# A decoder-trunk kernel: memory normalised and transposed in the input projection, attention outputs in DRAM per chunk, keys through five buffers, projection operands in a fixed order

## Chip, cores and metric

The kernel runs on one core of one Trainium2 chip. The metric is the device time of one execution in microseconds (us), lower is better.

## What is computed

One layer of a hybrid decoder over 2048 tokens of width 1024, in fp32. Cut to what matters here:

```python
mem_n = rms_norm(mem, mem_norm)                      # 256 memory tokens of width 1024
h = x + hybrid_mixer(rms_norm(x, mix_norm), ...)     # this pair of lines is stages 1, 2 and 3a
h = h + memory_cross_attention(rms_norm(h, cross_norm), mem_n, ...)   # stage 3
h = h + hierarchical_moe(rms_norm(h, moe_norm), ...)                  # stage 4
out = rms_norm(h, final_norm)

def hybrid_mixer(h, ...):
    fq, fk, fv, ff, gq, gk, gv, gg, ga = split(h @ w_in)
    fox = rms_norm(forgetting_attention(fq, fk, fv, ff + b_forget), fox_out_gain)   # 8 heads x 64, causal softmax
    gla = rms_norm(gla_chunked(gq, gk, gv, log_a), gla_out_gain) * silu(gg)         # 4 heads
    return concat(fox, gla) @ w_out

def memory_cross_attention(h, mem_n, ...):
    q, k, v = h @ w_xq, mem_n @ w_xk, mem_n @ w_xv
    return softmax(q k / sqrt(128)) v @ w_xo
```

## The kernel before

Fp32 products are made of fp32r halves: `split` (L58 to L72) writes a rounded part hi on ScalarE (ACT: L68, or L71 with a scale) and the rest lo on VectorE (DVE: L69, or L72), and `mm3` (L88 to L92) makes hi by hi, lo by hi and hi by lo on TensorE (PE: L90, L91, L92). A Tile scheduler sets the order of each engine's instructions; `issue_after` and `keep_in_program_order` bind it in places.

**Stage 1** (`stage1`, L129) normalises and transposes x in four chunks of 512 tokens (`prenorm`, and `turn` with its PE transposes L214), and multiplies by column groups of `w_in`: GQ and GK first, chunk by chunk with the next chunk's `turn` between the products, then GG, GV, FV, FQ and FK. From FV on the gated linear attention runs between them. FQ and FK end in `ttype` (L158): a PSUM tile `ps_mm` is split into two SBUF tiles from one ring of three (`tag="o1"`, L166), and four stores on SyncE's DMA queue (SP, L170) write the hi and lo of two heads to the DRAM tiles `qh_d`, `ql_d`, `kh_d`, `kl_d` of the chunk. The last group is FK, the keys.

**Stage 2** (`stage2`, L473) is the attention, in 16 units: p is a pair of heads, c a chunk of 512 queries. `load` (L492) fetches a unit's q and k halves (six DMAs of 256 to 272 KB) and, where p is 0, 256 KB of v; for p = 0 and c < 3 they are issued on GpSimd's queue (POOL), else on SP. `v1`, the 1 MB of v for the second pair, is always POOL's (L511). `maxima` (L513) finds each query's largest score: PE products `ps_a` (L525 and L526), DVE reductions (L528, and L530 for the diagonal block), a transpose `pmt` (L536), and a split of the negated maxima into `mh` and `ml`, which two POOL DMAs (L540) put into two rows of `q2`, in SBUF. `probs` then forms scores minus maxima (`ps_b`, L569 and L570, the second needs the rows just written), exponentials on ACT (L572) and the products with v. A unit's normalised output goes to the DRAM tensor `yT_d` (L620). In the last four units the generator `memory_in` (L771) runs beside them: it loads the gain broadcast over 128 partitions (L776) and two halves of the memory (L779), forms the sum of squares on ACT (L783), scales on DVE (L785), transposes on PE (L792) and copies to `mT` on DVE (L793).

**Stage 3a** (L685, `mixed` L701) is the output projection. Eight row blocks of `w_out` are loaded on SP (`wst`, L692) and split into `woh` (ACT) and `wol` (DVE). `enter(i)` loads 128 tokens of attention output `yT` (L719) and of gated linear attention output `y` (L720) and splits them into `yh` and `yl`; tile 0's loads are POOL's. `memory_out` (L803) forms the memory's keys (`ps_m`, L813) in between.

## Time and profile before

| | |
|---|---|
| runs | 2441.82, 2445.04, 2445.13 us, median 2445.04 |
| profiled execution | 2442.03 us, of which the span is 2440.3 us |
| PE busy | 2321.5 us, 95% of the span |
| DVE, ACT, POOL busy | 1433.6, 953.7, 678.7 us |
| granted clock of PE, mean over the span | 0.977 |
| DMA moved | 337.81 MB |

The span is what the profiler sees from the first to the last instruction; the profiled execution is 1.7 us longer. PE is busy nearly everywhere, so the table by itself tells little: what matters is where PE stands idle, what ended the idle time, and at what granted clock it went on (1.00 is 2.4 GHz, 0.50 is 1.2 GHz).

### The profile page before, as it was taken

To read this page: it belongs to the slowest core of one execution; us is meant where nothing else is said; L and a number is where in the kernel's file an instruction comes from. 1 tells how busy PE (TensorE), PEld (TensorE's weight loads), DVE (VectorE), ACT (ScalarE), POOL (GpSimd) and SP (SyncE) were. 2 spreads that over 40 slices of the span, in tenths; PEclk is the share of its full clock that TensorE was granted. 3 is DMA by queue.
4 is the path that set the end of the run, shared out by engine and by line. 5 is a ranking of instruction groups with operands and counts; after the bars stand their busy time and mean duration, and the time that the engine had idled before them with its cause. 6 is when DMAs were issued, how large, how long until landed. Compare 5 with 4: busy or idle time off the path is not lost. (4 is left out here: it accounts for less than half of the span.)

```text
span 2440.3 us, 39272 instructions
## 1 busy us (share of the span) xinstructions
PE 2321.5 (95%) x14569; PEld 1873.1 (77%) x14569; DVE 1433.6 (59%) x3561; ACT 953.7 (39%) x2058; POOL 678.7 (28%) x776
## 2 busy tenths in 40 slices
PE   7999999999979999999899999999599999999996
PEld 5778887777756656565488888887499989889985
DVE  5430035656527867877642255666568868778775
ACT  5321023434312434444431154554345545454542
POOL 2000002222134666665600001111332334223132
PEclk9999999999988999999999999999799999999998
DMA  5221222444484132312273422111678788779883
GB/s 181 72 90 66 77 83 83 127 111 133 109 204 98 49 92 63 83 42 77 70 245 115 143 82 70 49 40 56 184 242 265 229 286 248 260 215 274 262 246 116
DMA packets 281972, 337.81 MB, mean 138 GB/s; under 512 B 33766, under 2 KB 203296, under 8 KB 281775
## 3 DMA queue, kind: packets, MB, share of 16 engines
q1 hardware_dynamic: 248223, 246.73, 33.6%
q0 software_dynamic: 31248, 84.32, 11.8%
q10 hardware_dynamic: 2304, 4.20, 0.5%
q8 instruction: 116, 1.90, 0.3%
q14 instruction: 81, 0.66, 0.1%
HBM read 252.27 MB, written 93.02 MB: 141 GB/s over the span
## 5 line engine op out<-in xcount | busy, mean ns | idle before, releaser
L90 PE MATMUL gu<-xTh,wer 128*128 128x288 f32 x1024 | 304.7, 302 | 0.5 <-issue 0.5
L91 PE MATMUL gu<-xTl,wer 128*128 128x288 f32 x1024 | 304.1, 298 | 0.3 <-DVE xTl L69 0.3
L92 PE MATMUL gu<-xTh,wer 128*128 128x288 f32 x1024 | 303.1, 297 | 0.0
L69 DVE TENSOR_TENSOR wer<-wes,wer 128x1024 fp32r<-128x1024 f32 x192 | 232.5, 1222 | 37.1 <-ACT wer L68 36.9
L68 ACT ACTIVATE wer<-wes 128x1024 fp32r<-128x1024 f32 x192 | 197.9, 1052 | 118.5 <-PE yd L92 43.9
L572 ACT ACTIVATE pT<-ps_b 128x512 f32<-128x512 f32 (+3 forms) x320 | 158.8, 532 | 181.7 <-PE ps_b L570 161.8
L90 PEld LDWEIGHTS gu<-xTh,wer 128*128 128x128 f32 x1024 | 193.2, 190 | 3.7 <-ACT xTh L68 0.9
L91 PEld LDWEIGHTS gu<-xTl,wer 128*128 128x128 f32 x1024 | 194.2, 190 | 2.3 <-DVE xTl L69 0.9
L92 PEld LDWEIGHTS gu<-xTh,wer 128*128 128x128 f32 x1024 | 194.1, 190 | 1.8
L591 POOL TENSOR_TENSOR l<-l,pT 128x512 f32<-128x512 f32 (+3 forms) x128 | 153.6, 1200 | 53.9 <-ACT pT L572 47.5
L90 PE MATMUL ps_mm<-xh,w1r 128*128 128x512 f32 x384 | 153.4, 402 | 0.8 <-ACT w1r L71 0.5
L91 PE MATMUL ps_mm<-xl,w1r 128*128 128x512 f32 x384 | 153.4, 400 | 0.0
L92 PE MATMUL ps_mm<-xh,w1r 128*128 128x512 f32 x384 | 152.5, 399 | 0.1
L528 DVE TENSOR_REDUCE mm<-ps_a 128x1 f32<-128x512 f32 x192 | 128.2, 683 | 38.2 <-PE ps_a L526 37.6
L91 PE MATMUL ps_mm<-w1r,xh 128*128 128x512 f32 x384 | 150.1, 393 | 0.0
L92 PE MATMUL ps_mm<-w1r,xl 128*128 128x512 f32 x384 | 149.8, 392 | 0.0
L90 PE MATMUL ps_mm<-w1r,xh 128*128 128x512 f32 x384 | 148.3, 392 | 0.3 <-ACT o L186 0.3
L525 PE MATMUL ps_a<-k,q 128*128 128x512 f32 (+2 forms) x320 | 128.7, 404 | 18.9 <-DVE o L72 9.5
L556 PE MATMUL po<-pT,v 128*64 128x512 f32 (+3 forms) x640 | 131.7, 555 | 3.0 <-POOL pT L575 2.9
L569 PE MATMUL ps_b<-q,k 128*128 128x512 f32 (+3 forms) x320 | 125.2, 398 | 2.4 <-ACT pT L572 2.4
L591 DVE TENSOR_TENSOR l<-l,pT 128x512 f32<-128x512 f32 (+3 forms) x128 | 111.7, 873 | 23.3 <-ACT pT L572 11.6
L570 PE MATMUL ps_b<-q,k 68*128 68x512 f32 (+3 forms) x320 | 116.8, 376 | 4.1 <-DMA q<-ml 4.1
(431 smaller groups left out, 5622.0 us busy)
## 6 DMA issues: line engine op xcount, KB each, us to landing
wes<-in_w_expert_down_dram SPq DMA_DIRECT2D x64, 512.0 KB
wes<-in_w_expert_gate_dram SPq DMA_DIRECT2D x62, 512.0 KB
wes<-in_w_expert_up_dram SPq DMA_DIRECT2D x62, 512.0 KB
yr_d<-ye SPq DMA_DIRECT2D x32, 512.0 KB
w1s<-in_w_in_dram SPq DMA_DIRECT2D x48, 256.0 KB
xt<-in_x_dram SPq DMA_DIRECT2D x16, 512.0 KB
h_d<-x POOLq DMA_DIRECT2D x16, 512.0 KB
h<-h_d SPq DMA_DIRECT2D x16, 512.0 KB
```

Source lines behind the costliest of these rows:

```text
L68: nc.scalar.activation(hi, src, AF.Copy)
L69: nc.vector.tensor_tensor(lo, src, f32(hi), OP.subtract)
L90: mm(ps, ah, bh, start=start, stop=False)
L91: mm(ps, ah, bl, start=False, stop=False)
L92: mm(ps, al, bh, start=False, stop=stop)
L525: nc.tensor.matmul(ps[:, :w], q1[:, i, qs], k1[:, i, :w], start=True, stop=False)
L528: nc.vector.tensor_reduce(mm[:, i, b, j:j + 1], ps[:, :w], AX.X, OP.max)
L556: ins = nc.tensor.matmul(po[i * 64:i * 64 + 64, off:], V[p][:, kb, i * 64:i * 64 + 64], pts[i][:, off:], start=new and o == 0, stop=len(to ...
L569: nc.tensor.matmul(ps[:, off:], k1[:, i, ks], q1[:, i, off:], start=True, stop=False)
L570: nc.tensor.matmul(ps[:, off:], k2[0:68, i, ks], q2[0:68, i, off:], start=False, stop=True)
L572: nc.scalar.activation(pt[:, off:], ps[:, off:], AF.Exp)
L591: add(sums[i][:, off:], sums[i][:, off:], pt[:, off:], OP.add)
```

## The change

1. The memory is normalised in stage 1, beside the products of GQ and GK for the last chunk (`memory_norm`): the same sums of squares, a scaling without the gain, the same 16 transposes into the PSUM ring of `turn`, and 16 ACT copies of 128x128 that multiply by the gain as a column; four stores write `mT_d` in DRAM. In stage 2 `memory_in` is one load of `mT`.
2. `yT_d` is four DRAM tiles, one for each chunk of queries. The last unit writes its own from POOL. Tile 0's loads of stage 3a go to SP.
3. For the keys alone, lo takes a tile of the ring `w1s` (two), and hi keeps the ring `o1` (three).
4. The loads of the unit p = 0, c = 2 move from POOL to SP, and with them the 256 KB pieces of v for c = 2 and 3.
5. In stage 3a the weights 0 to 3 are split first, then the attention half of tile 0; the keys of the memory, the weights 4 to 7 and the other half of tile 0 are ordered behind it on ACT and DVE.

```diff
@@ stage1, ttype
-                    hi, lo = (op[0].tile([128, 512], F32R, tag="o1", name="o1", bufs=3) for _ in range(2))
+                    hi = op[0].tile([128, 512], F32R, tag="o1", name="o1", bufs=3)
+                    lo = wp.tile([128, 512], F32R, tag="w1s", name="o1", bufs=2) if parts[0] is self.kh_d else \
+                        op[0].tile([128, 512], F32R, tag="o1", name="o1", bufs=3)
@@ stage1, GQ and GK
-                    tn = turn(c + 1) if c < 3 else iter(())
+                    tn = turn(c + 1) if c < 3 else self.memory_norm(ip, px, lambda: op[0].tile([128, 512], F32, tag="o1", name="o1", bufs=n_o[0]))
@@ stage2, load
-                issue = nc.sync.dma_start if p or c == 3 else nc.gpsimd.dma_start
+                issue = nc.sync.dma_start if p or c > 1 else nc.gpsimd.dma_start
...
-                    nc.gpsimd.dma_start(V[p][:, b], self.fv_d[...])
+                    (issue if p == 0 else nc.gpsimd.dma_start)(V[p][:, b], self.fv_d[...])
@@ stage2, probs
-                nc.scalar.dma_start(self.yT_d[p * 128:p * 128 + 128, c * 512:(c + 1) * 512], o)
+                (nc.gpsimd if u is units[-1] else nc.scalar).dma_start(self.yT_d[c][p * 128:p * 128 + 128], o)
@@ mixed (weight(k) is the old loop's body: load wst, split into wh[k], wl[k])
+        for k in range(4):
+            split = weight(k)
...
-        for _ in enter(0):
-            pass
+        first = enter(0)
+        next(first)
+        with tc.issue_after(behind), tc.issue_after(done[0].ins), tc.issue_after(done[1].ins):
+            next(mem)
+            for k in range(4, KT):
+                weight(k)
+            next(first)
+            next(mem)
+        behind = self.loaded.ins
@@ memory
+    def memory_norm(self, ip, px, place):
...
+            nc.scalar.activation(jk, mt, AF.Square, accum_out=ss)
+            self.rstd(r, ss, 1.0 / D, ip)
+            nc.vector.tensor_scalar(mt, mt, r, None, op0=OP.mult)
+            xs.append(mt)
+        yield
+        for j, mt in enumerate(xs):
+            for h in range(2):
+                pt, o = px.tile([128, 4, 128], F32, name="pt_x"), place()
+                for q in range(4):
+                    k = 4 * h + q
+                    nc.tensor.transpose(pt[:, q], mt[:, k * 128:(k + 1) * 128], self.ident)
+                    nc.scalar.activation(o[:, q * 128:(q + 1) * 128], pt[:, q], AF.Copy, scale=self.gcol("mem_norm", k))
+                nc.sync.dma_start(self.mT_d[:, 4 * h:4 * h + 4, j * 128:(j + 1) * 128], o.rearrange("p (q t) -> p q t", q=4))
+            yield
+    def memory_in(self):
+        self.mT = self.mp.tile([128, KT, 256], F32, name="mT")
+        with self.tc.issue_after(self.loaded.ins):
+            self.nc.sync.dma_start(self.mT, self.mT_d)
+            self.ahead = [self.memory_weights(n) for n in range(2)]
+        yield
```

The order of the instructions moves in three places of interest. The first is SP's queue where stage 1 ends (`o` are the split keys of `ttype`; `kh_d_71` and `kl_d_75` belong to chunk 3). Before:

```order
L170 DMA kl_d_75<-o_6602 64x512 x2
L776 DMA mw<-in_mem_norm_dram 128x1024
L779 DMA mw<-in_mem_dram 128x1024
L170 DMA kh_d_71<-o_6634 64x512
L170 DMA kl_d_75<-o_6635 64x512
L170 DMA kh_d_71<-o_6634 64x512
L170 DMA kl_d_75<-o_6635 64x512
L496 DMA q_6760<-qh_d_63 64x2x512
L496 DMA q_6760<-ql_d_67 64x2x512
L496 DMA k_6758<-kh_d_71 64x2x512 x2
```

and in the change:

```order
L173 DMA kh_d_71<-o_6714 64x512 x2
L173 DMA kl_d_75<-o_6715 64x512 x2
L500 DMA q_6773<-qh_d_62 64x2x512
L500 DMA q_6773<-ql_d_66 64x2x512
L500 DMA k_6771<-kh_d_70 64x2x512 x2
L500 DMA q_6774<-qh_d_62 66x2x512
L500 DMA k_6772<-kl_d_74 68x2x512
L516 DMA v_6758<-fv_d 128x4x128
L500 DMA q_6840<-qh_d_63 64x2x512
```

The two memory loads are gone, and the seven loads of the unit c = 2 (`qh_d_62`, `kh_d_70`, the piece of v) stand between the last keys and the loads of the unit c = 3.

The second is DVE at the same place, from the last three low parts of the keys to the first masked maximum (`jk` and `mm` are the reduction's outputs). Before:

```order
L72 SCALAR_TENSOR_TENSOR o_6602<-ps_mm,o_6601 128x512
L72 SCALAR_TENSOR_TENSOR o_6635<-ps_mm,o_6634 128x512
L632 TENSOR_SCALAR causal<-jp 128x128
L81 TENSOR_SCALAR rs_v<-mss 128x1
L84 TENSOR_TENSOR rs_t<-rs_r 128x1
L85 SCALAR_TENSOR_TENSOR rs_t<-rs_t,rs_v 128x1
L86 SCALAR_TENSOR_TENSOR mr<-rs_t,rs_r 128x1
L785 SCALAR_TENSOR_TENSOR mw<-mw,mr 128x1024
L530 ISA jk,mm<-ps_a,causal 128x128
```

and in the change:

```order
L71 SCALAR_TENSOR_TENSOR o_6649<-ps_mm,o_6648 128x512
L71 SCALAR_TENSOR_TENSOR o_6682<-ps_mm,o_6681 128x512
L71 SCALAR_TENSOR_TENSOR o_6715<-ps_mm,o_6714 128x512
L637 TENSOR_SCALAR causal<-jp 128x128
L535 ISA jk,mm<-ps_a,causal 128x128
```

The five instructions of the memory's first half no longer stand between the last low part and the first maximum.

The third is DVE at the start of stage 3a (`wol` are the low parts of `w_out`, `kTl` those of the memory's keys, `yl` those of tile 0). Before:

```order
L69 TENSOR_TENSOR kTl<-ps_m,kTh 128x256
L72 SCALAR_TENSOR_TENSOR wol_11159<-wst,vcols,woh_11158 128x1024
L72 SCALAR_TENSOR_TENSOR wol_11165<-wst,vcols,woh_11164 128x1024
L69 TENSOR_TENSOR yl<-yT_11232,yh 128x512
L72 SCALAR_TENSOR_TENSOR wol_11171<-wst,vcols,woh_11170 128x1024
L72 SCALAR_TENSOR_TENSOR wol_11177<-wst,vcols,woh_11176 128x1024
```

and in the change:

```order
L71 SCALAR_TENSOR_TENSOR wol_11182<-wst,vcols,woh_11181 128x1024
L71 SCALAR_TENSOR_TENSOR wol_11188<-wst,vcols,woh_11187 128x1024
L71 SCALAR_TENSOR_TENSOR wol_11194<-wst,vcols,woh_11193 128x1024
L71 SCALAR_TENSOR_TENSOR wol_11200<-wst,vcols,woh_11199 128x1024
L68 TENSOR_TENSOR yl<-yT_11205,yh 128x512
L68 TENSOR_TENSOR kTl<-ps_m,kTh 128x256 x2
```

All four low parts of the first weights now stand ahead of tile 0's `yl`, and the memory's keys behind it.

## Rows read from the trace of the kernel before

**Rows 1.** What PE waited for, over the whole span: line and tile waiting, what ended the wait, us in total, times, longest.

```profile
PE ps_a L525 <- DVE o L72: 9.5, 1, 9.5
...
PE ps_a L525 <- DVE mm L530: 6.7, 3, 5.9
...
PE ps_b L570 <- DMA q<-ml: 4.1, 1, 4.1
```

**Rows 2.** Stretches from the end of stage 1 into stage 2: us, then busy time and instructions of PE, PE's weight loads, DVE, ACT and POOL, PE's granted clock, the busy share of the DMA engines and GB/s.

```profile
700.00:713.00 13.00, 13.00 (x60) 10.73 (x58) 1.94 (x6) 0.60 (x1) 5.82 (x12) 1.00 1.06 248
713.00:723.00 10.00, 0.48 (x3) 0.11 (x1) 1.51 (x3) 1.19 (x2) 0.00 (x0) 0.76 0.60 164
723.00:733.00 10.00, 4.12 (x13) 3.33 (x13) 3.06 (x11) 1.55 (x4) 1.47 (x3) 0.50 0.99 273
733.00:743.00 10.00, 9.43 (x28) 7.32 (x26) 8.06 (x27) 0.27 (x1) 1.08 (x2) 0.54 1.05 206
743.00:753.00 10.00, 6.43 (x22) 5.80 (x23) 3.42 (x10) 2.66 (x6) 3.93 (x10) 0.66 0.46 126
```

**Rows 3.** ACT in order of time, the last two high parts of the keys: start, us, instruction, and in brackets the idle time before it and what ended it.

```profile
717.46 0.60 ACT L71 ACTIVATE o<-ps_mm 128x512 fp32r<-128x512 f32 x1 [12.34 <-DMA kl_d<-o]
721.52 0.60 ACT L71 ACTIVATE o<-ps_mm 128x512 fp32r<-128x512 f32 x1 [3.46 <-DMA kl_d<-o]
```

**Rows 4.** DVE in order of time: the last two low parts of the keys, the memory's scaling behind them, the low part of the first unit's maxima, and the last reduction of the unit c = 1.

```profile
719.53 0.69 DVE L72 SCALAR_TENSOR_TENSOR o<-ps_mm,o 128x512 fp32r<-128x512 f32 x1 [10.34 <-DMA kh_d<-o]
722.15 0.69 DVE L72 SCALAR_TENSOR_TENSOR o<-ps_mm,o 128x512 fp32r<-128x512 f32 x1 [1.93 <-ACT o L71]
...
729.02 0.15 DVE L81 TENSOR_SCALAR rs_v<-mss 128x1 f32<-128x1 f32 x1 [6.05 <-ACT sq L783]
...
730.26 1.28 DVE L785 SCALAR_TENSOR_TENSOR mw<-mw,mr 128x1024 f32<-128x1024 f32 x1
...
738.59 0.27 DVE L72 SCALAR_TENSOR_TENSOR ml<-pmt,mh 8x128 fp32r<-8x128 f32 x1
...
755.02 0.17 DVE L534 TENSOR_REDUCE m<-mm 128x8 f32<-128x16 f32 x1
```

**Rows 5.** PE in order of time: the last matmul of stage 1, the first two groups of maxima, and the first matmul behind the third wait.

```profile
712.99 0.39 PE L92 MATMUL ps_mm<-xh,w1r 128*128 128x512 f32 x1
722.89 1.12 PE L525 MATMUL ps_a<-k,q 128*128 128x128 f32 x3 [9.52 <-DVE o L72]
...
731.81 0.79 PE L525 MATMUL ps_a<-k,q 128*128 128x512 f32 x1 [5.88 <-DVE mm L530]
...
746.57 1.51 PE L570 MATMUL ps_b<-q,k 68*128 68x512 f32 x3 [4.10 <-DMA q<-ml]
```

**Rows 6.** POOL in order of time: the first load of the unit c = 2, the 1 MB of v for the second pair of heads, and the two DMAs of the maxima.

```profile
698.66 0.62 POOL L496 DMA_DIRECT2D q<-qh_d  x1 [0.24 <-DMA v<-fv_d]
...
729.82 1.16 POOL L511 DMA_DIRECT2D v<-fv_d  x1 [18.16 <-DMA q<-qh_d]
...
739.30 0.54 POOL L540 DMA_DIRECT2D q<-ml  x1
```

**Rows 7.** SP in order of time: two stores of a tile's high keys, the last store of stage 1, and the first load behind it.

```profile
705.15 1.11 SPq L170 DMA_DIRECT2D kh_d<-o  x2
...
724.34 0.60 SPq L170 DMA_DIRECT2D kl_d<-o  x1
724.99 0.62 SPq L496 DMA_DIRECT2D q<-qh_d  x1
```

**Rows 8.** PE in order of time in stage 2's last units: the memory's transposes.

```profile
1106.47 0.60 PE L792 MATMUL pt<-ident,mw 128*128 128x128 f32 x4
...
1117.49 0.60 PE L792 MATMUL pt<-ident,mw 128*128 128x128 f32 x4
...
1128.73 0.63 PE L792 MATMUL pt<-ident,mw 128*128 128x128 f32 x4 [0.90 <-DVE mw L785]
...
1133.19 1.06 PE L792 MATMUL pt<-ident,mw 128*128 128x128 f32 x4
```

**Rows 9.** Two stretches around the last two of them, columns as in rows 2.

```profile
1126.00:1132.00 6.00, 4.45 (x19) 2.82 (x18) 5.96 (x11) 0.00 (x0) 1.59 (x3) 0.94 0.31 87
1132.00:1136.00 4.00, 4.00 (x17) 3.28 (x16) 2.69 (x7) 2.23 (x5) 1.76 (x2) 0.67 0.28 98
```

**Rows 10.** PE in order of time from stage 2 into stage 3a.

```profile
1199.56 7.07 PE L813 MATMUL ps_m<-mT,mw 128*128 128x256 f32 x32
1212.26 0.80 PE L90 MATMUL ps<-woh,yh 128*128 128x512 f32 x1 [5.63 <-ACT yh L68]
...
1214.13 4.84 PE L813 MATMUL ps_m<-mT,mw 128*128 128x256 f32 x16
```

**Rows 11.** DVE in order of time at the same place: the last small operation, the first two low parts of the weights, and `yl`.

```profile
1206.61 0.35 DVE L1081 COPY same<-same 128x32 f32<-128x32 f32 x3
...
1208.12 2.48 DVE L72 SCALAR_TENSOR_TENSOR wol<-wst,vcols,woh 128x1024 fp32r<-128x1024 f32 x2 [0.61 <-ACT woh L71]
1212.24 0.69 DVE L69 TENSOR_TENSOR yl<-yT,yh 128x512 fp32r<-128x512 f32 x1 [1.64 <-ACT yh L68]
```

**Rows 12.** ACT in order of time in stage 3a: the fifth block of the weights.

```profile
1216.51 1.15 ACT L71 ACTIVATE woh<-wst,vcols 128x1024 fp32r<-128x1024 f32 x1 [2.22 <-DMA wst<-in_w_out_dram]
```

**Rows 13.** Stage 1 while the last chunk meets GQ and GK, columns as in rows 2.

```profile
120.00:140.00 20.00, 20.00 (x89) 16.19 (x88) 4.98 (x7) 5.15 (x8) 0.00 (x0) 1.00 0.11 39
```

More of the change, by code (lines that the diff above doesn't have):

```diff
@@ L494, in load, with dma @@
                 p, c = u["p"], u["c"]
-                issue = nc.sync.dma_start if p or c == 3 else nc.gpsimd.dma_start
-                dma = lambda out, src: issue(f32(out), src.rearrange("h d s -> d h s"))
+                issue = nc.sync.dma_start if p or c > 1 else nc.gpsimd.dma_start
+                def dma(out, src):
+                    self.loaded = issue(f32(out), src.rearrange("h d s -> d h s"))
                 hs = slice(2 * p, 2 * p + 2)
@@ L510, in load @@
                     b = slice(4 * c, 4 * c + n)
-                    nc.gpsimd.dma_start(V[p][:, b], self.fv_d[b.start * 128:b.stop * 128, p * 128:p * 128 + 128].rearrange("(b k) d -> k b d", k=128))
+                    (issue if p == 0 else nc.gpsimd.dma_start)(V[p][:, b], self.fv_d[b.start * 128:b.stop * 128, p * 128:p * 128 + 128].rearrange("(b k) d -> k b d", k=128))
             def maxima(u):
@@ L687, in stage3a, with mixed, weight @@
                 tc.tile_pool(name="ps3a", bufs=2, space=PSUM, reuse_waits="tile") as pp:
-            mem = self.memory_out(pp)
-            wh, wl = [], []
-            for k in range(KT):
-                st = (wp if k % 4 < 2 else ip).tile([128, D], F32, tag=("wst", "x3")[k % 4 // 2], name="wst", bufs=2)
-                self.loaded = self.nc.sync.dma_start(st, a["w_out"].rearrange("l k n -> (l k) n")[k * 128:(k + 1) * 128])
-                for ws, nm in ((wh, "h"), (wl, "l")):
-                    ws.append((wp, wp2)[k // 4].tile([128, D], F32R, name=f"wo{nm}{k}"))
-                self.split(wh[k], wl[k], st, self.gcol("fox_out_gain", k) if k < 4 else self.gcol("gla_out_gain", k - 4))
-                if k % 4 == 3:
-                    next(mem)
-            self.mem = mem
-            self.mixed(wh, wl, ip, wp, pp)
-    def mixed(self, wh, wl, ip, wp, pp):
-        nc = self.nc
+            self.mixed(ip, wp, wp2, pp)
+    def mixed(self, ip, wp, wp2, pp):
+        nc, tc, a = self.nc, self.tc, self.a
+        mem = self.memory_out(pp)
+        wh, wl = [], []
+        def weight(k):
+            st = (wp if k % 4 < 2 else ip).tile([128, D], F32, tag=("wst", "x3")[k % 4 // 2], name="wst", bufs=2)
+            self.loaded = nc.sync.dma_start(st, a["w_out"].rearrange("l k n -> (l k) n")[k * 128:(k + 1) * 128])
+            for ws, nm in ((wh, "h"), (wl, "l")):
+                ws.append((wp, wp2)[k // 4].tile([128, D], F32R, name=f"wo{nm}{k}"))
+            return self.split(wh[k], wl[k], st, self.gcol("fox_out_gain", k) if k < 4 else self.gcol("gla_out_gain", k - 4))
+        for k in range(4):
+            split = weight(k)
         x = self.a["x"].rearrange("b s d -> (b s) d")
@@ L706, in mixed @@
         behind = self.loaded.ins
-        tiles = {}
+        tiles, done = {}, []
         def enter(i):
@@ L792, in memory_in @@
                     nc.tensor.transpose(pt[:, q], mt[:, k * 128:(k + 1) * 128], self.ident)
-                nc.vector.tensor_copy(mT[:, 4 * h:4 * h + 4, j * 128:(j + 1) * 128], pt)
-                yield
-        self.ahead = [self.memory_weights(n) for n in range(2)]
+                    nc.scalar.activation(o[:, q * 128:(q + 1) * 128], pt[:, q], AF.Copy, scale=self.gcol("mem_norm", k))
[7 more added lines that the diff above has]
+        yield
     def memory_weights(self, n):
```

45 lines of the change are left out of this document (18 added, 27 removed).

## The prediction

> **What bounds the kernel now.** PE is busy for 2321.5 us of the 2440.3 us span, so an edit helps where it shortens PE's idle time, its time at half clock, or its own work. I read PE's waits first, then short windows around the longest of them, then the single engines in order of time. Three waits stand one behind the other where stage 1 passes into stage 2 [rows 1]: 9.5 us of `ps_a` for a low part of the keys, 5.9 us of `ps_a` for DVE, and 4.1 us of `ps_b` for the DMA of `ml`. A fourth, 5.6 us for `yh`, opens the output projection [rows 10]. The windows show their second cost [rows 2]: PE ran at clock 1.00 to 713 and stood nearly still for 10 us; then the granted clock was 0.50 and 0.54, the lower of its two levels (1.2 GHz), and 0.66 in the next window.
>
> The cause of the first wait is a ring of three buffers. The last two high parts of the keys waited 12.34 and 3.46 us and the low part between them 10.34 us, all for stores of older tiles [rows 3, 4]. The stores of high keys issued at 705.15 [rows 7] freed the buffer only at 719.5, some 14 us later, in a stretch where the DMA share was 1.06 [rows 2]. PE's last matmul of stage 1 had ended at 713.4 [rows 5]. The second wait is DVE's order: the memory's first half waited 6.05 us for its sum of squares, scaled for 1.28 us, and only then came the masked maxima [rows 4]. The third is the way of 4 KB through a full queue: `ml` went out at 739.30 and `ps_b` started at 746.57 [rows 5, 6].
>
> **Part by part, stage 1 to stage 2.** Hi now has three buffers and lo two. A tile has 24 matmuls; 60 took 13.00 us [rows 2], so a tile takes at least 5.2 us, a lo buffer is asked for again after 10 us at the earliest and a hi buffer after 16, against the 14 us of a store at the worst load. I take the last lo as ready one hi and one lo after the last matmul: 713.4 + 0.60 + 0.69 = 714.7 in place of 722.84, so 8.1 us of the 9.5 go (bounds: 4 if a store still takes 14 us and lo waits for it, 8.1 else). The second wait goes whole, 5.9 us, since nothing stands there on DVE; the masked reductions that follow are of 0.3 to 0.7 us, and there is no third user in the order.
>
> The third wait is late next. From the first `ps_a` to `ml` on POOL took 739.30 − 722.89 − 5.88 = 10.5 us at half clock [rows 5, 6]; I take 9, since DVE paces part of it, which gives an issue at 724. Ahead of it POOL issues the 1 MB of `v1`, which waits until stage 1's last buffers are stored: it went out 5.5 us after the last store of the keys [rows 6, 7], so now at some 721. In a full queue `ml` took 7.3 us, and part of the 1 MB is ahead of it: at the 206 to 273 GB/s of [rows 2], shared with SP, 1 MB takes 4 to 10 us. I let `ml` land at 733. So `ps_b` starts at 733 in place of 746.6: **−13.6 us**. Bounds: −16.6 if `ml` is issued after 8 us and lands in 7.3; −8 if only the DMA engines decide, since what they can gain is their 40% of idle time from 713 to 723, 4 us, and the two memory loads of 1 MB that are gone, 4 to 5 us.
>
> Moving the loads of the unit c = 2 from POOL to SP takes 1.85 MB out of the stretch from 698.66 on, in which the stores of the keys took 14 us [rows 6, 7], and puts it behind the last key. This is what makes me take the upper value for the first wait. Here a rule speaks against me. The Trainium skill ("DMA: Bandwidth & Descriptors", section "Issuing engines are not separate DMA queues") says that DMAs started by SP, ACT or GpSimd run on the same 16 engines and interleave, and that several issuers only save issue time. By it the bytes of the passage stay what they were, and the gain stays at the DMA bound, −8; the share of 0.60 between 713 and 723 speaks for more, because the moved bytes fill a hole there. The price of the move: these loads are now issued from 717 on, at SP's pace of some 0.6 us each [rows 7]. PE asks for them when the maxima of c = 1 are done, which was at 755.0, 8.5 us behind the start of `ps_b` [rows 4, 5]; that would be 741 now. At 206 GB/s their 1.85 MB take 9 us, with `v1` beside them 14, until 731; I cost the move at nothing, and if that cover fails, at up to 5 us.
>
> **The memory's move.** Stage 2 loses four groups of transposes, 0.60 + 0.60 + 0.63 + 1.06 = 2.9 us [rows 8], and the idle time around the last two: 6.00 − 4.45 = 1.55 us, of which 0.90 is named as DVE's scaling; the 4 us at clock 0.67 behind it cost 1.3 us [rows 9]. Together −5.8 at most; I take −5, since not all idle time need be the memory's. Stage 1 gains the same 16 transposes at full clock, 4 × 0.60 = +2.4 us, since PE is busy for 20.00 of 20 us there [rows 13]. The squares, the scaling and the 16 small ACT copies (each under the 0.60 of a 128x512 one [rows 3], so 9.6 us at most) lie beside PE: ACT is busy 5.15 and DVE 4.98 of 20 us [rows 13]. The trace does not show how PE fares when a group of four transposes waits for a PSUM buffer that ACT empties in four steps: between 0 and one group of copies, 2.4 us. I take 0, for PE has products to do between. The four stores and the load of 1 MB meet DMA shares of 0.11 and 0.31 [rows 9, 13]. Sum **−2.6** (bounds −3.4, and +1.9 if no idle time goes and PE waits once).
>
> **Stage 3a.** The load of `yT` no longer waits for the last unit, so `yh` is not late. What is late next is `yl`: on DVE the four low parts come first. They start at about 1207, behind the small operations, and take 2.48 for two [rows 11]: 1207 + 5.0 + 0.69 = 1212.6, while PE stood from 1206.6 to 1212.26 [rows 10]. PE can do two products and four transposes, about 1.5 us, ahead of that wait. So the 5.6 us shrink little: **−1**. The bounds are −3 (no time at half clock behind it) and +6: the eighth block of `w_out` is loaded only when the seventh is split, and a load then took until 1216.51 to be usable with ACT waiting 2.22 us for it [rows 12]; a chain of two could leave PE without weights for as long as this wait, 5.6 us.
>
> **Sum.** −13.6 − 2.6 − 1 = −17.2, on the profiled execution of 2442.03: 2424.8, say **2425 us**. That execution lies 3.0 us below the median of the runs and 0.2 above the lowest of them, so I keep the sum there; against the median it would be 2428. The smallest difference that a measurement of this kernel can tell is about 0.2%, 4.9 us.
>
> **Rivals.** (a) *The DMA engines give the third wait what the first two lose.* The same bytes in a shorter stretch: `ml` behind `v1` lands at 738, and the unit c = 2 arrives 3 us late. For it: shares of 0.99 and 1.05 [rows 2]. Against it: the hole of 713 to 723. The passage then gains 746.6 − 738 − 3 = 5.6, stage 3a nothing, and the time is 2442.0 − 5.6 − 2.6 = 2434. The rule of the Trainium skill above would come out here. (b) *Most of it is taken back in stage 3a and stage 1*: the passage as in (a), the weight chain at +6 and one wait for a PSUM buffer at +2.4 make 2442.0 − 5.6 − 2.6 + 2.4 + 6 = 2442, no change. (c) *Slower: the unit c = 2 is late.* Its loads stand on SP behind the last keys, while those for c = 3 and `v1` compete. Each us that they land behind 741 costs one, so it decides from 17.2 us on, at 758; landing at 766, it makes 2425 + 25 = 2450. Against it: 1.85 MB from 717 to 758 is 45 GB/s, and the stretches with a share of 0.99 and more show 206 to 273 [rows 2]. (d) *The five buffers don't release the split*, because the lo ring of two is shared with the weights' loads; these have all been read by then, so it would only wait for its own stores. This is the bound of 4 above, and (a) covers it.
>
> **How the numbers follow.** My forecast 0.55, with a range of its own of 2416 to 2432; (a) and (d) 0.28; (b) 0.10; (c) 0.07. Faster by over 0.2% holds the first two, 0.83; within it (b), 0.10; slower (c), 0.07. The range of 8 in 10 reaches from 2415 (all terms at their good bounds make 2442 − 16.6 − 3.4 − 3 = 2419, and some 4 us more would go with part of the half clock between 733 and 753, [rows 2]) over (a) with stage 3a at its bad bound, 2434 + 6: to 2440.
>
> **What would show it.** Right: the high and low keys at the end of stage 1 wait under 2 us for their stores; the first `ps_a` waits 1 to 2 us; no wait of `ps_a` for L535 over 1 us; `ps_b` waits 4 to 8 us for `ml`, and starts about 20 us after the last matmul of stage 1 in place of 33; no transposes of the memory in stage 2; PE at 20.00 of 20 in stage 1; in stage 3a a wait for `yl` of about 4 us. Wrong: a wait of `ps_a` for DMAs of the unit c = 2, a wait of `ps_b` over 9 us, a lo that still waits 8 us for its buffer, or a wait for `wol` in stage 3a.

## The result, and the profile after

The change made the kernel slower: 2457.66 us (median of five runs, 2455.41 to 2462.22) against 2441.82 us for the kernel before beside it (2437.20 to 2445.13). The ratio is 1.0063, 95% interval 1.0051 to 1.0076. The forecast was 2425 us, and its range ended at 2440. The profiled execution took 2455.41 us, with a span of 2453.7 us at a mean granted clock of 0.978; before, the span was 2440.3 us at 0.977.

First, what PE waited for in the kernel after, over the whole span, sorted by the total (line and tile waiting, what ended the wait, us in total, times, longest); these answer to [rows 1]:

```profile
PE ps_b L574 <- ACT pT L577: 5.7, 4, 3.1
PE ps_a L530 <- DVE mm L533: 5.4, 6, 2.8
PE ps_mm L90 <- DVE o L157: 5.0, 1, 5.0
PE ps_b L575 <- DMA q<-ml: 4.5, 2, 3.1
...
PE ps L90 <- DVE kTl L68: 2.4, 1, 2.4
PE pt_x L803 <- ACT o L804: 2.4, 3, 1.3
...
PE ps_a L530 <- DVE o L71: 1.4, 1, 1.4
```

The three waits of [rows 1] shrank: the 9.5 us for a low part of the keys are 1.4, the 5.9 us behind the memory's scaling are gone (the longest wait of `ps_a` for DVE now lies elsewhere and is 2.8), and the first wait for `ml` is 1.48 of the 4.5 us in the fourth line, less than the 4 to 8 us of the forecast. New are a wait of 5.0 us of `ps_mm` in stage 1, three of `pt_x` that make 2.4 us together, a second one for `ml`, and 2.4 us for `kTl`; the longest one for `pT` grew from 1.3 to 3.1 us. None of them is for the loads of the unit c = 2.

Five markers in the order of PE's work show where the time went. The table gives, for one profiled execution of each kernel, how much longer (+) or shorter (−) than before each part took, in us. Stage 1 ends here with the last gated output `y` of the linear attention (700.13 us before); the passage ends with the first `ps_b` of L575 (746.57); the first unit ends with its output (774.61); the rest of stage 2 ends with the first `ps_m` (1199.56); stage 3a ends with the first product of stage 3b (1420.86), and the part behind it with the issue of the last store of the output. The kernels other than after are those of the experiments.

| kernel | stage 1 | passage | first unit | rest of stage 2 | stage 3a | behind | all |
|---|---|---|---|---|---|---|---|
| after | +10.2 | −13.4 | +2.5 | +8.3 | +3.7 | +2.8 | +14.1 |
| own_ring | +0.9 | −12.8 | +6.4 | +6.0 | +4.1 | −0.6 | +4.1 |
| fe_o2 | +11.1 | −12.7 | +5.2 | +0.9 | +4.6 | +1.2 | +10.3 |
| stage3a_old | +11.8 | −14.2 | +3.4 | +6.3 | +3.2 | +0.5 | +11.0 |
| keys_only | −2.8 | −0.5 | −0.1 | +0.2 | 0.0 | −1.9 | −5.0 |
| held_loads | +2.6 | −12.9 | +8.7 | +2.6 | +2.3 | +1.5 | +4.7 |
| unit2_pool | −0.1 | −3.5 | +1.0 | +6.8 | +3.9 | +3.2 | +11.2 |
| mem_stage2 | −4.2 | −6.5 | +7.0 | +4.3 | +2.8 | +2.8 | +6.2 |
| parts134 | 0.0 | −12.9 | +3.3 | +1.0 | −0.2 | −2.4 | −11.2 |
| memory_only | +13.8 | −4.7 | −0.6 | +2.3 | +0.4 | +1.2 | +12.4 |
| memory_xt | +3.6 | −6.3 | +2.6 | −1.6 | −1.3 | +2.3 | −0.7 |
| stage3a_only | −1.4 | −0.4 | +0.2 | −3.4 | +1.7 | +2.6 | −0.8 |
| late_p1 | +1.5 | −12.0 | +3.2 | +4.0 | +0.7 | +0.9 | −1.8 |
| ring_fe2 | 0.0 | −12.7 | +4.7 | −2.7 | +1.4 | +3.2 | −6.1 |
| before_fe2 | −2.7 | −1.3 | −0.1 | −4.7 | +0.5 | +0.5 | −7.7 |
| parts134_fe2 | +2.5 | −13.3 | +5.2 | −5.1 | +0.4 | +1.9 | −8.4 |

Single executions of one kernel differ (parts134 ran between 2430.2 and 2449.5 us, and before_fe2 has −2.7 in stage 1, where its code is that of the kernel before), so a cell of 2 or 3 us says little; the verdicts come from the medians, and the table tells where to look. In its first row, the passage gained what was forecast, and stage 1, stage 2 and stage 3a lost more than that.

**Stage 1.** Two windows of the kernel before, columns as in [rows 2], and below them the same two of the kernel after:

```profile
140.00:150.00 10.00, 10.00 (x45) 6.59 (x45) 3.04 (x5) 3.18 (x6) 0.00 (x0) 1.00 0.45 141
150.00:160.00 10.00, 10.00 (x46) 8.29 (x45) 8.28 (x28) 4.07 (x7) 0.18 (x1) 1.00 0.40 110
```

```profile
140.00:150.00 10.00, 8.95 (x41) 5.67 (x40) 3.37 (x5) 4.12 (x9) 0.00 (x0) 1.00 0.61 184
150.00:160.00 10.00, 3.43 (x14) 1.97 (x13) 2.95 (x4) 4.76 (x12) 0.00 (x0) 0.78 0.57 159
```

The kernel after in order of time, on ACT, DVE, SP and PE (start, us, instruction; in brackets the idle time before it and what ended it):

```profile
130.54 0.37 ACT L804 ACTIVATE o<-pt_x,vcols 128x128 f32<-128x128 f32 x1 [3.18 <-DMA gqk_d<-o]
...
158.50 0.69 DVE L157 COPY o<-ps_mm 128x512 f32<-128x512 f32 x1 [1.95 <-DMA mT_d<-o]
...
156.05 0.93 SPq L805 DMA_DIRECT2D mT_d<-o  x2
...
159.24 0.79 PE L90 MATMUL ps_mm<-w1r,xh 128*128 128x512 f32 x1 [5.03 <-DVE o L157]
159.84 0.63 PE L91 MATMUL ps_mm<-w1r,xh 128*128 128x512 f32 x1
```

Read from below: PE stands 5.03 us because DVE has not emptied a PSUM tile; DVE stands because its output tile `o` is still being stored, and the store is that of the memory, `mT_d`. The scaled copies of the memory take their tile from the ring `o1` (two buffers in this part of stage 1), in which the results of GQ and GK go out as well. The first ACT row shows the other direction: the memory's copy waits for a store of `gqk_d`. Behind the wait a product takes 0.63 us where it took 0.39: the window's granted clock is 0.78. The first product of GG, at 148.76 us before, starts 10.5 us late.

**The end of stage 2.** In order of time on SP, ACT and PE of the kernel after:

```profile
1097.46 0.38 SPq L812 DMA_DIRECT2D mT<-mT_d  x1
1097.88 5.37 SPq L820 DMA_DIRECT2D mw<-in_w_xk_dram  x2
1107.92 5.77 SPq L703 DMA_DIRECT2D wst<-in_w_out_dram  x4
...
1112.60 0.33 ACTq L625 DMA_DIRECT2D yT_d<-fe_o  x1
...
1118.41 0.60 ACT L604 ACTIVATE fe_o<-po 128x512 f32<-128x512 f32 x1 [4.35 <-DMA yT_d<-fe_o]
...
1119.55 0.80 PE L574 MATMUL ps_b<-q,k 128*128 128x512 f32 x1 [3.15 <-ACT pT L577]
```

and the windows of the same place:

```profile
1105.00:1110.00 5.00, 5.00 (x26) 2.49 (x25) 2.44 (x5) 2.61 (x5) 2.69 (x3) 1.00 1.05 243
...
1115.00:1120.00 5.00, 1.85 (x8) 1.43 (x8) 1.75 (x3) 1.59 (x4) 0.92 (x2) 0.81 0.63 247
1120.00:1125.00 5.00, 5.00 (x14) 1.72 (x15) 3.47 (x5) 1.07 (x2) 3.56 (x5) 0.51 0.00 0
```

The transposes of [rows 8] are gone, and with them what had spread the loads: all of `mT`, `mw` and `wst` now goes out between 1097 and 1114 us (before, the two `mw` went out from 1128.61 and the four `wst` from 1134.71). The store of a unit's output, issued at 1112.60, lands behind them: it is 5.81 us until ACT writes its buffer again. For the same unit it was 3.98 us in the kernel before:

```profile
1108.23 0.33 ACTq L620 DMA_DIRECT2D yT_d<-fe_o  x1
...
1112.21 0.60 ACT L599 ACTIVATE fe_o<-po 128x512 f32<-128x512 f32 x1 [1.88 <-DMA yT_d<-fe_o]
```

There is one buffer `fe_o`; in the kernel after ACT waits 4.35 us for it with the next exponentials queued behind, PE waits 3.15 us for these, and then runs 5 us at a granted clock of 0.51, the lower level. Before, PE did not wait here.

**The passage and stage 3a** stand with the experiments that bear on them.

### The profile page after: what moved, and what is told of

Same layout as the page of the kernel before. It is cut to its first block, busy times and chain, and to the rows that moved or that the text cites. A ratio compares the mean times of both kernels' runs of the same rounds, so it can differ in the third digit from the quotient of the medians.

```text
span 2453.7 us, 39282 instructions
## 1 busy us (share of the span) xinstructions
PE 2328.0 (95%) x14569; PEld 1869.8 (76%) x14569; DVE 1432.2 (58%) x3557; ACT 960.5 (39%) x2074; POOL 666.8 (27%) x767
## 5 line engine op out<-in xcount | busy, mean ns | idle before, releaser
L575 PE MATMUL ps_b<-q,k 68*128 68x512 f32 (+3 forms) x320 | 115.9, 374 | 4.5 <-DMA q<-ml 4.5
```

The source lines that it names most:

```text
L575: nc.tensor.matmul(ps[:, off:], k2[0:68, i, ks], q2[0:68, i, off:], start=False, stop=True)
```

## The experiments

Ratios are against the kernel before on the same chip in the same batch (2438.84 to 2441.24 us), with 95% intervals.

### The two buffers

**own_ring**: the memory's scaled copies get tiles of the ring `xt` (4 KB a partition, two halves) in place of `o1`.

```diff
         for j, mt in enumerate(xs):
+            out = ip.tile([128, D], F32, name="xt", bufs=4)
             for h in range(2):
-                pt, o = px.tile([128, 4, 128], F32, name="pt_x"), place()
+                pt, o = px.tile([128, 4, 128], F32, name="pt_x"), out[:, 512 * h:512 * h + 512]
```

> The changed kernel, with the memory's scaled copies in tiles of the ring xt in stage 1 instead of the ring o1 that the products' results pass through. Theory ring: in stage 1 the copies hold one of two o1 buffers from the first of four small ACT copies to the end of a store, so results of GQ and GK wait, PSUM fills and PE stops (5.0 us for DVE L157, a further 2.4 us for ACT L804, half clock behind it). Then the first product of GG starts 2 to 4 us later than in the kernel before instead of 10.5 later, and the time falls by 6 to 9 us against the changed kernel, to about 2450. Rival copies: ACT's sixteen small copies or SP's queue of late weight loads are the cause; then GG still starts 8 to 11 us late and the time stays at 2457.

Measured: 2446.81 us, 1.0027 (1.0016 to 1.0038). Some 8.8 us of the kernel after's loss is this ring (1.0063 − 1.0027 of 2440). Stage 1's windows show it:

```profile
140.00:150.00 10.00, 10.00 (x47) 6.62 (x46) 3.68 (x5) 4.52 (x10) 0.00 (x0) 1.00 0.69 208
150.00:160.00 10.00, 10.00 (x48) 8.12 (x47) 6.56 (x21) 4.65 (x9) 0.18 (x1) 1.00 0.40 112
```

PE is busy throughout at full clock, with the same sixteen copies on ACT and the same four stores (DMA shares of 0.69 and 0.40, against 0.61 and 0.57 in the kernel after). The first product of GG starts at 149.90, 1.1 us late in place of 10.5. The kernel is still slower than before, so the ring is not all.

**fe_o2**: on the kernel after, two buffers for the unit's output.

```diff
-                t = lambda nm: fp.tile(..., bufs=1)
+                t = lambda nm: fp.tile(..., bufs=2 if nm == "o" else 1)
```

> The changed kernel, with two buffers instead of one for the attention output fe_o that is stored to yT_d. Theory store: in the last units the loads of mT and w_out, now issued at 1097 to 1113 instead of 1118 to 1137, fill the DMA engines while a unit's output is stored; ACT waits 4.4 us for the store to free fe_o, holds back the exponentials behind it, and PE stops for 3.2 us at 1119 and goes on at half clock. With a second buffer ACT does not wait for the store, and the stretch from the twelfth to the fifteenth unit's output is 4 to 7 us shorter; the time falls by 3 to 7 us to about 2452. Rival: DVE or POOL set the pace there, ACT only happens to stand behind the store; then the time stays within 2 us of 2457.

Measured: 2449.57 us, 1.0038 (1.0022 to 1.0054): a quarter of a per cent back. In the table the rest of stage 2 is +0.9 where after has +8.3. ACT's waits that ended with this store, in total, times and longest, in the kernels before and after; fe_o2 has none:

```profile
ACT fe_o L599 <- DMA yT_d<-fe_o: 6.6, 4, 2.3
```

```profile
ACT fe_o L604 <- DMA yT_d<-fe_o: 23.3, 5, 7.2
```

Not all of these totals is the store. The longest in the kernel after, 7.18 us, ended at 1138.99, and its store was issued at 1136.90: for 5.1 us ACT waited for the output to be formed. Nor is it new that such a wait reaches PE: in the kernel before, the longest one (2.35 us, ended at 884.20) is followed by 1.32 us of PE waiting for `pT` at 885.33. The change made the one beside the loads longer.

**ring_fe2**: both edits on the kernel after. **before_fe2**: the second edit alone on the kernel before, to see what of its gain has nothing to do with the change.

> The kernel of own_ring with two buffers for fe_o. Theory store: own_ring's ACT waits 7.2 us for the store of the twelfth unit's output and PE 3.2 us, with half clock behind it; with the second buffer this goes and the time falls by 4 to 7 us against own_ring's 2447 (ratio 1.0027 to the kernel before), to a ratio of 0.9995 to 1.001. Rival: what fe_o2 gained came from its other order; then the ratio stays at 1.002 to 1.003.

> The kernel before with two buffers for fe_o. Theory store: ACT waits 2.3 us at the longest for a store there and PE not at all, so the buffer gives 0 to 2 us, a ratio of 0.999 to 1.0005. Rival: a second fe_o buffer helps whatever the loads do, as units overlap more; then the ratio is 0.996 to 0.998.

Measured: ring_fe2 2437.71 us, 0.9981 (0.9968 to 0.9994); before_fe2 2437.81 us, 0.9991 (0.9977 to 1.0005), which no one can tell from no change. So by the medians the second buffer is worth 0.46%, 11 us, on top of own_ring, 0.25% on the kernel after, and 0.09% on the kernel before (0.23% at most). Windows of ring_fe2 around the loads and stores, which stand there some 17 us earlier than in the kernel after:

```profile
1075.00:1095.00 20.00, 20.00 (x102) 12.32 (x101) 14.98 (x29) 10.07 (x22) 15.19 (x27) 1.00 0.82 202
1095.00:1115.00 20.00, 20.00 (x100) 13.11 (x98) 17.33 (x31) 9.63 (x21) 15.07 (x20) 1.00 0.31 116
```

PE has no idle time and no half clock left there. With both buffers given, the changed kernel is 0.19% faster than the kernel before. That this is a gain of the change is not shown: before_fe2 has the second buffer and nothing of the change, and the two can't be told apart (0.9981 and 0.9991).

### The memory's move

**memory_only**: part 1 alone on the kernel before, as the change makes it. **memory_xt**: the same with own_ring's tiles, and with the loads held as in held_loads, below. **mem_stage2**: on the kernel after, part 1 alone undone (the memory is normalised and transposed in stage 2 as before).

> The kernel before with the memory's move alone, as the change makes it: scaled copies through the ring o1, loads of mT and w_out not held. Theory: this one part makes the whole loss; GG starts 8 to 11 us late, the twelfth unit's store is late as well, and only the wait behind the memory's scaling goes; the time is 2450 to 2458, that is 10 to 18 us slower than the kernel before. Rival: the loss comes of the parts together (the loads on SP, the keys, stage 3a), and the move alone costs under 6 us.

> The kernel before with the memory's move alone, mended in two places: scaled copies in the ring xt, and the load of mT held until the thirteenth unit's output is formed. Theory: the forecast's term for the move (2.6 us gained, and 5.9 us of the wait behind the memory's scaling) was right apart from the two things mended, so the time is 2 to 8 us under the kernel before. Rival: what the passage gains is taken back within stage 2, as in own_ring and held_loads, and the time is within 3 us of the kernel before.

> The changed kernel with the memory normalised and transposed in stage 2 as in the kernel before; all other parts of the change stay. Theory: the move costs what stage 1 loses (10.5 us at the first product of GG), so undoing it puts GG at 0 to the kernel before; the memory's scaling stands on DVE ahead of the first maxima again, which takes back up to 6 us at the passage to stage 2; the time is 2446 to 2452. Rival: the memory's move is a gain apart from the ring, so undoing it leaves the time at 2455 or above.

Measured: memory_only 2458.36 us, 1.0084 (1.0071 to 1.0097); memory_xt 2438.13 us, 1.0000 (0.9992 to 1.0009); mem_stage2 2445.74 us, 1.0018 (1.0005 to 1.0031). The move alone is enough for the whole loss. PE in memory_only waits in stage 1 as the kernel after does,

```profile
160.41 0.80 PE L90 MATMUL ps_mm<-w1r,xh 128*128 128x512 f32 x1 [5.34 <-DVE o L157]
```

and waits 3.06 us for `pT` at 1122.65, beside the early loads. With other tiles and later loads the move costs nothing, but neither does it give the 2.6 us of the forecast or anything of the 5.9 us of the wait behind the scaling (its interval allows 2.0 at most). mem_stage2 shows the other side: the first `ps_a` waits 1.41 us as in the kernel after, the wait behind the memory's scaling is back with 6.90 us, the loads of `mw` go out from 1127.06, and ACT's longest wait that ends with a store of `fe_o` is 2.8 us. Yet its rest of stage 2 is +4.3 in the table, which nothing here explains. And without the move the rest of the change is still not a gain.

**held_loads**: own_ring, and the load of `mT`, with the four `wst` behind it on SP, is held until a late unit's output has been formed (the two `mw` were not held).

```diff
+        for _ in range(13):
+            yield
+        with self.tc.issue_after(last[0].ins):
+            self.nc.gpsimd.memset(self.mT[:, 0, 0:1], 0.0)
         with self.tc.issue_after(self.loaded.ins):
```

> The kernel of own_ring, with the load of mT held until the thirteenth unit's output is formed (a small GpSimd memset of mT in that place, on which the load waits; the loads of w_out stand behind it on SP). Theory store: DMA engines filled at 1100 to 1110 by these loads delay the store of the twelfth unit's output, ACT waits 7.2 us for it, PE 3.2 us, and half clock follows. With the loads held the wait of PE at 1112 goes, the first ps_m comes 4 to 7 us earlier than in own_ring (which had it at +0.5 to the kernel before), and the time is 2440 to 2443 against 2447. Rival: the time that this place loses belongs to ACT's and DVE's order after the memory's work is gone; then PE still waits for pT there, and the time stays at 2446 or more.

Measured: 2441.86 us, 0.9997 (0.9982 to 1.0012), against own_ring's 1.0027. In its trace the loads of `w_out` go out 22 us later than in own_ring (1122.71 for 1100.21), and the collision has moved with them (SP and ACT):

```profile
1122.71 2.12 SPq L703 DMA_DIRECT2D wst<-in_w_out_dram  x4
...
1125.07 0.33 ACTq L625 DMA_DIRECT2D yT_d<-fe_o  x1
1132.63 0.60 ACT L604 ACTIVATE fe_o<-po 128x512 f32<-128x512 f32 x1 [12.64 <-DMA yT_d<-fe_o]
```

ACT waits 12.64 us for the buffer, and the last 7.56 of them are the store of 256 KB. Most of it lies where PE has other work; 3.40 us of PE, ended at 1134.40, stand behind it. The medians say that holding the loads helps; this execution, 2446.17 us and above the median, does not show by which step.

### The passage

**keys_only**: part 3 alone on the kernel before (five buffers for the split keys). **unit2_pool**: own_ring with part 4 undone, so that the unit c = 2 is loaded from POOL, early.

```diff
-                issue = nc.sync.dma_start if p or c > 1 else nc.gpsimd.dma_start
+                issue = nc.sync.dma_start if p or c == 3 else nc.gpsimd.dma_start
...
```

> The kernel before with one part of the change: the five buffers for the keys. Theory part sum: the first wait at the passage to stage 2 falls from 9.5 to under 3 us, while the wait of 5.9 us behind the memory's scaling stays and may grow, since the two memory loads land no earlier; ps_b starts 3 to 8 us earlier and the time is 2434 to 2439 against 2442. Rival: five buffers alone don't help, since the stores still take 14 us next to the loads of the unit c = 2 on POOL; then the first wait stays over 6 us and the time within 2 us of 2442.

> The kernel of own_ring with the loads of the unit c = 2 and of v back on GpSimd's queue, ahead of the last keys. Theory hole: moving these loads behind the last keys is what lets the keys' stores land early, so undoing it brings a wait of 3 to 8 us of the first ps_a back, and ps_b starts 3 to 8 us later than in own_ring (which had it 11.9 us earlier than the kernel before); the time is 2449 to 2453. Rival engines: which queue issues them does not matter, since the same engines carry the same bytes; ps_b starts within 2 us of own_ring. A third way: the second unit's ml finds empty DMA engines, its wait of 2.3 us goes, and the time falls below 2445.

Measured: keys_only 2437.57 us, 0.9993 (0.998 to 1.0006); unit2_pool 2447.97 us, 1.0035 (1.0022 to 1.0048), against own_ring's 1.0027. PE's first wait in keys_only, where it was 9.52 us before:

```profile
720.40 1.11 PE L527 MATMUL ps_a<-k,q 128*128 128x128 f32 x3 [7.98 <-DVE o L72]
```

PE in own_ring, the waits of the passage and of the unit behind it:

```profile
717.33 0.67 PE L530 MATMUL ps_a<-k,q 128*128 128x128 f32 x3 [1.41 <-DVE o L71]
...
734.72 1.51 PE L575 MATMUL ps_b<-q,k 68*128 68x512 f32 x3 [2.17 <-DMA q<-ml]
...
757.80 0.94 PE L575 MATMUL ps_b<-q,k 68*128 68x512 f32 x3 [2.25 <-DMA q<-ml]
```

and in unit2_pool:

```profile
723.56 1.11 PE L530 MATMUL ps_a<-k,q 128*128 128x128 f32 x3 [8.52 <-DVE o L71]
...
742.98 1.51 PE L575 MATMUL ps_b<-q,k 68*128 68x512 f32 x3 [6.28 <-DMA q<-ml]
...
762.11 0.94 PE L575 MATMUL ps_b<-q,k 68*128 68x512 f32 x3 [0.30 <-DMA q<-ml]
```

With the unit's 1.85 MB in the way of the stores, the five buffers alone leave a first wait of 7.98 us (keys_only) and 8.52 us (unit2_pool): the loads have to move too, as the prediction argued. That brings the first `ps_b` forward by 8.3 us. But at the second `ml`, the third row of each, the distance is 4.3 us, and at the end the two medians can't be told apart (their intervals overlap). The bytes that are moved out of the stores' way come some 20 us later (the first at 719 us in own_ring, at 698.66 before [rows 6]), and the loads behind them on SP come later too: the last of the second pair's keys that are loaded in this stretch go out at 751.83 in own_ring, at 745.89 in unit2_pool. The second `ml` goes out at 751.58 in own_ring.

The Trainium skill ("DMA: Bandwidth & Descriptors", section "Issuing engines are not separate DMA queues") says that transfers from different issuing engines share the same 16 engines, so that the choice saves only issue time. The end of the kernel does not speak against it (1.0027 and 1.0035), the passage does (8.3 us), since on SP the bytes stand behind the last keys and are issued later.

**parts134**: held_loads, with stage 3a and the last unit's store as before. **late_p1**: parts134, and the loads of the second pair's keys wait for the first unit's `ml`, to clear the way of the second.

```diff
+                if p == 1:
+                    with tc.issue_after(self.max_dma.ins):
+                        for t in (k1, k2):
+                            nc.gpsimd.memset(f32(t)[:, 0, 0:1], 0.0)
```

> The kernel of held_loads with stage 3a entirely as in the kernel before, its last store on ScalarE and tile 0's loads on GpSimd included. Theory: the new order of stage 3a costs 3.7 to 4.1 us from the first ps_m to its end, so this kernel is 3 to 5 us faster than held_loads: 2436 to 2439, faster than the kernel before by 1 to 4 us. Rival: stage 3a costs the same in both orders once stage 2 ends as it does now (the old order with the last store on GpSimd cost 3.2 us); then the time is within 2 us of held_loads.

> The kernel of parts134 with the loads of the second pair of heads held: two small GpSimd memsets of each key tile, behind the DMAs of the second unit's maxima (and of the next units' for the next tiles). Theory sink: what the passage gains is lost again at the second unit's ml, which takes 6 to 7 us beside these loads; held, the wait of ps_b of 2.7 us near 755 falls under 1 us, PE stays at full clock, and the time falls by 2 to 5 us to about 2436. Rival: the path of ml over GpSimd takes that long without loads as well, and the wait stays over 2 us; the time stays within 2 us of parts134, or grows if a unit of the second pair waits for its keys.

Measured: parts134 2439.63 us, 1.0004 (0.9991 to 1.0017); late_p1 2438.22 us, 0.9996 (0.9985 to 1.0007). Neither can be told from the kernel before. late_p1's second wait for `ml` is gone, but the first grew:

```profile
736.02 1.19 PE L579 MATMUL ps_b<-q,k 68*128 68x512 f32 x2 [5.91 <-DMA q<-ml]
```

against 1.86 us in parts134. `ml` itself took about as long, 9.35 us from its issue at 726.67 to its use, against 8.81 in parts134: PE had 3 us less work ahead of the wait in the new order. With the second pair's keys out of the way the DMA share from 750 to 755 is 0.07 (0.68 in parts134) and the second wait is gone, but nothing that can be told at the end was gained.

### Stage 3a

**stage3a_only**: parts 2 and 5 on the kernel before. **stage3a_old**: on the kernel after, stage 3a's order and the loads of tile 0 as before (`yT_d` stays in four tiles, and the last store stays on POOL).

> The kernel before with yT_d as four tiles, the last unit's store on GpSimd and the new order of stage 3a; nothing else. Theory: yl waits behind four low parts of the weights (3.7 us against 5.6 before), the memory's keys wait 2.4 us behind late weights, and stage 3a loses 2 to 4 us from the first ps_m to its end, as in the changed kernel; the time is 2441 to 2444 against 2439 to 2440. Rival: the loss there belonged to the DMA traffic that the memory's move shifts; alone the order gains 0 to 2 us.

> The changed kernel with stage 3a as in the kernel before: the order of the operands and tile 0's loads, yT_d still as four tiles. Theory order: the new order costs 3.7 us (a wait of 3.7 us for yl behind four low parts of the weights, and one of 2.4 us for the memory's keys behind weights that come late); undoing it gives back 3 to 5 us, about 2453. Rival: the new order gains 1 us as forecast and the loss has come from what stage 2 leaves behind; then undoing it costs 1 to 3 us, about 2459.

Measured: stage3a_only 2443.55 us, 1.0023 (1.001 to 1.0035): slower by itself. stage3a_old 2452.68 us, 1.0058 (1.0041 to 1.0076): no repair. PE of stage3a_only:

```profile
1207.09 0.79 PE L92 MATMUL ps<-woh,yl 128*128 128x512 f32 x1 [3.69 <-DVE yl L68]
...
1226.75 0.50 PE L90 MATMUL ps<-woh,yh 128*128 128x512 f32 x1 [2.29 <-DVE kTl L68]
```

and of stage3a_old:

```profile
1222.53 0.80 PE L90 MATMUL ps<-woh,yh 128*128 128x512 f32 x1 [8.60 <-ACT yh L68]
```

The new order trades the one wait of 5.63 us [rows 10] for 3.69 and 2.29. stage3a_old is a mixture that neither kernel has: its load of `yT` stands on POOL behind the last store, and `yh` comes later than in the kernel before or after. It tells little of part 5. The table does: the eight kernels with the new stage 3a, after among them, have +1.4 to +4.6 there, the seven with the old one −1.3 to +0.7. In the medians the cost shows in stage3a_only alone: where only stage 3a and the last store are put back, from held_loads to parts134 (0.9997 and 1.0004) and from ring_fe2 to parts134_fe2 (0.9981 and 0.9972, below), the intervals overlap.

### The best of them

**parts134_fe2**: own_ring and two buffers `fe_o`, with stage 3a and the last store as before.

> The kernel of own_ring with two buffers for fe_o and stage 3a, its last store and tile 0's loads as in the kernel before. Theory: both losses are mended, so what is left of the passage's gain shows: 3 to 7 us faster than the kernel before, a ratio of 0.997 to 0.999. Rival sink: the gain at the passage is taken back behind it (the second unit's ml, the clock), and the ratio is 0.9995 or above.

Measured: 2435.04 us (2430.47 to 2436.93), 0.9972 (0.9961 to 0.9984). It beats both kernels, by 0.28% (6.8 us) against the kernel before and by more against the kernel after, and is the one version whose ratio is more than the 0.2% under 1 that the prediction took as the smallest difference to be told. How much of that is the change's is open, for before_fe2 (0.9991) has the second buffer too, and the two intervals overlap. It keeps parts 1, 3 and 4 of the change and puts back parts 2 and 5, but for the four tiles of `yT_d`.

## Why the prediction was wrong, point by point

**The passage, −13.6: right in mechanism and size.** From the last matmul of stage 1 to the first `ps_b` it was 33.2 us before, and the prediction asked for about 20. In the kernel after, PE's last product starts at 724.86 us, and then:

```profile
726.66 0.67 PE L530 MATMUL ps_a<-k,q 128*128 128x128 f32 x3 [1.41 <-DVE o L71]
...
743.37 1.51 PE L575 MATMUL ps_b<-q,k 68*128 68x512 f32 x3 [1.48 <-DMA q<-ml]
...
764.52 0.93 PE L575 MATMUL ps_b<-q,k 68*128 68x512 f32 x3 [3.06 <-DMA q<-ml]
```

which makes 18.1 us. `ml` was issued at 734.99, 8.3 us after the first `ps_a` (the prediction took 9), and took 8.4 to be usable (7.3 before); PE had so much other work ahead of it that it waited 1.48 us of these, not 4 to 8. Each step is shown: keys_only and unit2_pool leave the first wait at 7.98 and 8.52 us without the move of the loads, and mem_stage2 has the second back with 6.90 us. What the sum lacked is the last row. The prediction ended at the first `ps_b`, as if a unit that starts 13.6 us early also ended so. The second unit's `ml` meets the loads that had been moved, waits 3.06 us, and a stretch at a clock of 0.83 follows (0.62 and 0.53 in the windows from 730 on). The first unit's output stands 2.5 us later against the passage's gain, 3 to 9 us in the other kernels with this passage. This is rival (a) in part: its mechanism, that the DMA engines give the time back, at the second `ml` in place of the first. In the medians the best of the kernels with both buffers keeps 6.8 us of the forecast's 17.2, with a second `fe_o` that was no part of it.

**Stage 1, +2.4: the first step that failed, by 8 us.** "Between 0 and one group of copies, 2.4 us. I take 0, for PE has products to do between." The prediction looked at the PSUM ring `pt_x`, which ACT empties in four steps, and had its wait, 2.4 us in all. It did not ask from which ring the copies' SBUF tile comes and who else waits for one. A tile of `o1` is held from the first of the four copies to the landing of its store; that the copies lie beside PE, with ACT busy 5.15 of 20 us [rows 13], says nothing of how long the tile is held. own_ring shows it (−0.36%), memory_only shows it alone (1.0084).

**Stage 2, −5: failed, by 13 us in the table's one execution, by some 11 in the medians (own_ring to ring_fe2).** The prediction took the move's loads as free: "The four stores and the load of 1 MB meet DMA shares of 0.11 and 0.31." The load was costed by the share of the old windows at the old place [rows 9]. But the memory's work had been what kept the loads of `mw` and `w_out` back; without it all of them go out at once, 27 us and more earlier, and the share there is 1.05. The transposes' 2.9 us did go. What came in their place is the wait for the single `fe_o`. fe_o2 and ring_fe2 show it, and mem_stage2, without the move, has neither the early loads nor the wait of PE; before_fe2 shows that by the medians most of it is the change's (0.46% against 0.09%), though the intervals leave room for less. A wait of 2.77 us of PE at 836.85 is part of the 8.3 us in the trace of after and belongs to no term of the forecast, see the last section.

**Stage 3a, −1: failed, by about 5 us in the table's one execution, inside its bounds of −3 and +6.** The wait for `yl` came as forecast, 3.68 us for the "about 4". In order of time on DVE, PE and ACT of the kernel after:

```profile
1214.21 4.86 DVE L71 SCALAR_TENSOR_TENSOR wol<-wst,vcols,woh 128x1024 fp32r<-128x1024 f32 x4
...
1219.73 0.80 PE L92 MATMUL ps<-woh,yl 128*128 128x512 f32 x1 [3.68 <-DVE yl L68]
...
1239.80 0.50 PE L90 MATMUL ps<-woh,yh 128*128 128x512 f32 x1 [2.39 <-DVE kTl L68]
...
1223.37 1.15 ACT L70 ACTIVATE woh<-wst,vcols 128x1024 fp32r<-128x1024 f32 x1 [8.07 <-DMA wst<-in_w_out_dram]
```

What was missing is what waits behind the ordered operands. The first block of the second half of `w_out` reaches ACT after 8.07 us of waiting, where the block in its place had waited 2.22 [rows 12]; ACT waits for the blocks behind it too, the last of `w_out` comes at 1233.24, and at 1237.22 ACT still waits 2.31 us for a block of `w_xq`; DVE splits `kTl` behind that block's low parts, and PE waits again. It is the bound that the prediction named (a weight chain of two) with another victim.

**The rivals.** (c), slower because the unit c = 2 is late, did not happen: there is no PE wait for its loads. Nor did (d): the last high parts of the keys wait for PE and no longer for a store (4.84 us for `ps_mm`, the last at 725.28). (b) was nearest, the gain taken back in stage 1 and stage 3a, but it priced stage 1 at 2.4 us and left stage 2 a gain. The sum of the mis-sized terms is what turns −17 into the +14 of the table: in the table's one execution 8 in stage 1, 13 in the rest of stage 2, 5 in stage 3a, 2.5 behind the passage, and 2.8 in the last stages, which no experiment explains and which is within what two executions of a kernel differ by.

**What stays open**: why own_ring's first unit gives back 6.4 us and held_loads' 8.7 where after gives back 2.5; by which step holding the loads gains 0.3%; and whether keys_only is a small gain or none.

## What to carry to other kernels

When work moves to a place where every engine has time, list the buffers that it takes there, who else takes from that ring, and for how long one is held: from the first write to the landing of the store, not for the busy time of the instruction. When work is taken away, ask what it had been holding back, and cost the transfers at the time at which they will now be issued. And follow a gain past the first wait that it shortens, to the next transfer of the same kind, before it goes into the sum.

## What the runs showed that was not expected

The same store of 256 KB holds its buffer for very different times. In held_loads, issued behind 3 MB of loads (`mT` and four `wst`), it was 7.56 us until ACT wrote the buffer again; in the kernel after, issued some 23 us behind the last of them, it was 2.09:

```profile
1136.90 0.33 ACTq L625 DMA_DIRECT2D yT_d<-fe_o  x1
1138.99 0.60 ACT L604 ACTIVATE fe_o<-po 128x512 f32<-128x512 f32 x1 [7.18 <-DMA yT_d<-fe_o]
```

The same two rows show that a wait put down to a store can be mostly a wait for what is stored: 5.1 of the 7.18 us lie ahead of the issue.

One instruction on DVE took far longer than usual. In the kernel after, on DVE and POOL:

```profile
831.71 4.49 DVE L593 TENSOR_TENSOR l<-pT 128x512 f32<-128x512 f32 x1
...
834.36 4.64 POOL L596 TENSOR_TENSOR l<-l,pT 128x512 f32<-128x512 f32 x3
```

The median of this line's 16 instructions on DVE is 0.69 us; this one took 4.49, and the maximum behind it kept PE waiting 2.77 us at 836.85. fe_o2, stage3a_old and late_p1 have it at the same place with 4.47 to 4.48 us; in the other traces no instruction of this line takes over 1.8. POOL runs back to back beside it, but does so in the kernel before as well (828.45 to 838.15), where it took 0.92. No experiment was made on it, so the cause is open.
